# A decoder block in compensated fp32r: the second feed-forward block by seven block products, its hidden through memory, its last pass token tile by token tile

## The chip, the core and the metric

The kernel runs on one core of one Trainium2 chip. The metric is the device time of one execution in microseconds. A profiled execution gives, for the same core, the span from the first to the last instruction and a trace of every instruction: TensorE (PE, and PEld for its weight loads), VectorE (DVE), ScalarE (ACT), GpSimd (POOL) and SyncE (SP), whose queue issues most of the DMAs.

## What is computed

One sequence of 1024 tokens, width 1024, passes one decoder block and a final norm; d_ff is 2752:

```python
def rms_norm(x, g):
    return x * lax.rsqrt(jnp.mean(x * x, -1, keepdims=True) + EPS) * g
def swiglu(x, w_gu, w_down):
    gate, up = jnp.split(x @ w_gu, 2, axis=-1)
    return (jax.nn.silu(gate) * up) @ w_down

h = x
h = h + 0.5 * swiglu(rms_norm(h, ffn1_norm), ffn1_w_gu, ffn1_w_down)
h = h + hybrid_mixer(rms_norm(h, mix_norm), ...)      # sparse attention + HGRN2, then @ w_out
h = h + 0.5 * swiglu(rms_norm(h, ffn2_norm), ffn2_w_gu, ffn2_w_down)
return rms_norm(h, final_norm)
```

Everything is float32. The mixer's attention compresses keys and values in blocks of 32 tokens (`compress`), selects blocks, and has a window branch; the change touches its norm, its compression and the second half of its `w_out`.

## The kernel before

**A product.** TensorE multiplies in fp32r. Each fp32 operand is split into a high part and a rest (`split`, L134: the high part on POOL or ACT, the rest on DVE, L137 to L141), and each product is three matmuls, high by high, high by low, low by high (`mm3`, L143; the lines L145, L146, L147). A matmul has 128 x 128 weights and 512 columns in the feed-forward blocks.

**Tiles.** Tokens go in two halves of 512, or 8 tiles `tt` of 128. d_ff goes in 22 column tiles `j` of 128, the last 64 wide; a tile j has a gate and an up part. Plain, one j costs 2 parts x 2 token halves x 8 contraction tiles x 3 = 96 matmuls.

**FFN1** computes j = 0 to 2 plain (`up_plain`, L503), j = 3 to 20 by seven block products of the 2 x 2 blocks (contraction halves by token halves) (`up_strassen`, L561: 84 matmuls per j), j = 21 by `up_last`. The seven products need combined x operands, XO 0 to 6 (`x_sums`), built once, and combined weight pieces, built per j on DVE and POOL (`up_pieces`), and their results are combined by DVE. `up_out` (L493) multiplies by the norm factor R, applies silu and stores the hidden (`hs`) to memory by SP (L501). The second half, `down` (L594), makes four passes (token half x column half) over the 22 j; each pass reloads the hidden (L605) and w_down (L607), splits both, and accumulates four results; j = 0 and 1 are prepared in memory of their own ahead of the first pass. The norm of FFN1 needs each token's sum of squares: ACT squares xt, DVE adds (L215), 16 one-column matmuls sum over partitions (L221), rsqrt (L156 to L168), and L243 spreads the factors.

**Norms elsewhere** (`norm_rows`, L176): four whole-tile squares on ACT (L182), a rsqrt of 12 small DVE steps, four scaled tiles `xn` (DVE L192 twice, ACT, POOL L190), then transposes on TensorE (L201).

**FFN2** uses `ffn` (L324): chunks of two j, gate and up plain, the hidden stays on the chip; per chunk 16 results (8 token tiles x 2 column halves) of up to 6 matmuls (L405 to L407), each added to h by DVE (L409). After the last chunk come squares, rsqrt and output per token tile (L1426 to L1439).

**Order.** A scheduler sets the order within each engine from data and buffers; each engine then runs its list in that order, and a DMA queue too. So what stands behind a waiting instruction waits with it.

## Time and profile before

| what | value |
|---|---|
| median of 3 runs | 2183.11 us (2182.26 to 2185.56) |
| profiled execution, its own time | 2181.18 us |
| its span | 2179.5 us |
| mean granted TensorE clock | 0.995 |
| busy: PE, DVE, ACT, POOL | 98%, 57%, 27%, 21% |
| FFN1's first half ends, `down` ends | 438 us, 686 us |
| FFN2 starts, its last chunk's products start | 1451 us, 2140 us |

Engines run side by side and wait for each other by semaphores; a busy share is a mean over all stages. In a timeline row stand start, duration, engine, line, operation, what it writes and reads, and in brackets the idle time of that engine before it with what ended it. xN behind a row says that N like instructions are shown as one. A matmul's duration is longer than the distance from one start to the next, since matmuls are pipelined.

### The profile page before, as it was taken

The numbers are of one execution on the slowest core, as the hardware profiler recorded it, in microseconds if no ns is written. First come the engines' busy times: TensorE is split into PE (matmuls) and PEld (weight loads), VectorE is DVE, ScalarE is ACT, GpSimd is POOL, SyncE is SP. The second block draws the span as 40 slices with busy tenths as digits, with TensorE's granted clock in tenths as the row PEclk, the third lists the DMA queues.
The fourth block names the chain that finished last, engine by engine and source line by source line (L and its number), as shares of the span: only waits on it lengthen the run. The fifth ranks groups of instructions, "written<-read, shape, count | busy, mean of one in ns | idle before, by whom it ended". The sixth has DMA issues, their size and how long they took to land.

```text
span 2179.5 us, 29005 instructions
## 1 busy us (share of the span) xinstructions
PE 2134.0 (98%) x10866; PEld 1743.3 (80%) x10866; DVE 1231.6 (57%) x2560; ACT 589.6 (27%) x1270; POOL 461.7 (21%) x515
## 2 busy tenths in 40 slices
PE   8999999999999999999999999999999999999996
PEld 6888888878887889999866766698888888888884
DVE  8965555456775556556589776374333434333436
ACT  5532333222323111221576554330000000000003
POOL 2222223232231000001255333121010101010103
PEclk9999999999999999999999999999999999999998
DMA  5322222076773211100101111331111111111101
GB/s 174 98 77 78 87 88 82 34 292 194 229 239 105 81 39 40 42 20 20 39 20 38 41 42 37 131 117 57 40 46 52 49 49 58 40 48 49 45 9 78
DMA packets 87277, 169.14 MB, mean 78 GB/s; under 512 B 9792, under 2 KB 31328, under 8 KB 87136
## 3 DMA queue, kind: packets, MB, share of 16 engines
q1 hardware_dynamic: 85840, 163.07, 23.3%
q10 hardware_dynamic: 1296, 4.21, 0.5%
q8 instruction: 86, 1.41, 0.3%
q14 instruction: 55, 0.45, 0.1%
HBM read 145.49 MB, written 21.76 MB: 77 GB/s over the span
## 4 chain that ended last, share of the span: by engine, by line
PE 89%; DVE 6%; issue 2%; DMA 1%; ACT 1%; POOL 0%; SPq 0%; DVEq 0%; POOLq 0%; ACTq 0%
PE b L145 16%; PE b L147 16%; PE b L146 16%; PE b L1062 4%; PE b L620 4%; PE b L619 3%; PE b L618 3%; PE b L407 3%; PE b L405 3%; PE b L406 3%; PE b L1072 3%; PE b L638 2%; PE b L640 2%; PE b L639 2%; PE b L727 2%
## 5 line engine op out<-in xcount | busy, mean ns | idle before, releaser
L145 PE MATMUL b<-xT,wh 128*128 128x512 f32 x944 | 371.2, 394 | 0.8 <-DVE qa L921 0.7
L146 PE MATMUL b<-xT,wh 128*128 128x512 f32 x944 | 368.4, 390 | 0.0
L147 PE MATMUL b<-xT,wl 128*128 128x512 f32 x944 | 368.4, 390 | 0.0
L137 POOL TENSOR_SCALAR wh<-wr 128x1024 fp32r<-128x1024 f32 (+2 forms) x86 | 87.1, 1027 | 735.4 <-PE b L146 525.1
L145 PE MATMUL b<-xT,wp 128*128 128x512 f32 x584 | 228.4, 392 | 2.1 <-ACT pp L523 2.1
L146 PE MATMUL b<-xT,wp 128*128 128x512 f32 x584 | 228.1, 391 | 0.5 <-DVE xT L427 0.5
L147 PE MATMUL b<-xT,wp 128*128 128x512 f32 x584 | 227.8, 390 | 0.0
L341 DVE TENSOR_TENSOR sg<-b,sg 128x512 f32<-128x512 f32 (+1 forms) x44 | 30.4, 692 | 331.9 <-PE b L147 322.3
L147 PEld LDWEIGHTS b<-xT,wl 128*128 128x128 f32 x944 | 177.3, 188 | 37.4 <-issue 0.8
L145 PEld LDWEIGHTS b<-xT,wh 128*128 128x128 f32 x944 | 177.3, 188 | 36.0 <-POOL P L1041 0.8
L146 PEld LDWEIGHTS b<-xT,wh 128*128 128x128 f32 x944 | 177.5, 188 | 34.7
L141 DVE TENSOR_TENSOR dw<-dr,dw 128x512 fp32r<-128x512 f32 x172 | 133.5, 812 | 77.4 <-ACT dw L139 65.9
L409 DVE SCALAR_TENSOR_TENSOR g<-b,g 128x512 f32<-128x512 f32 x176 | 118.4, 685 | 59.8 <-PE b L407 59.6
L620 PE MATMUL b<-dw,dw 128*128 128x512 f32 x352 | 137.7, 391 | 0.2 <-DVE dw L141 0.2
L618 PE MATMUL b<-dw,dw 128*128 128x512 f32 x336 | 132.5, 394 | 5.1 <-POOL dw L137 4.3
L619 PE MATMUL b<-dw,dw 128*128 128x512 f32 x352 | 137.5, 391 | 0.0
L406 PE MATMUL b<-dh,hh 128*128 128x512 f32 x352 | 137.0, 389 | 0.0
L407 PE MATMUL b<-dl,hh 128*128 128x512 f32 x352 | 137.0, 389 | 0.0
L1041 POOL TENSOR_SCALAR P<-P,sm,gate 128x640 f32<-128x640 f32 (+7 forms) x128 | 106.3, 841 | 142.9 <-DVE sm L1039 138.8
L405 PE MATMUL b<-dh,hl 128*128 128x512 f32 x336 | 131.2, 390 | 5.1 <-DVE g L409 5.1
L141 DVE TENSOR_TENSOR wl<-wr,wh 128x1024 fp32r<-128x1024 f32 (+2 forms) x86 | 118.7, 1387 | 27.7 <-POOL wh L137 25.1
L1037 ACT ACTIVATE P<-P,sm 128x64 f32<-128x64 f32 (+8 forms) x192 | 114.8, 600 | 65.3 <-DVE sm L1002 57.0
(277 smaller groups left out, 4103.2 us busy)
## 6 DMA issues: line engine op xcount, KB each, us to landing
wr<-in_ffn_w_gu_dram SPq DMA_DIRECT2D x82, 512.0 KB, 3.7
dr<-in_ffn_w_down_dram SPq DMA_DIRECT2D x126, 256.0 KB, 3.1
dr<-hs SPq DMA_DIRECT2D x84, 256.0 KB, 3.1
hs<-sg SPq DMA_DIRECT2D x42, 256.0 KB, 2.2
wr<-in_w_in_dram SPq DMA_DIRECT2D x20, 512.0 KB, 5.0
wr<-in_w_out_dram SPq DMA_DIRECT2D x20, 256.0 KB, 3.1
xf<-in_xt_dram SPq DMA_DIRECT2D x16, 256.0 KB, 5.0
h<-in_x_dram SPq DMA_DIRECT2D x8, 512.0 KB, 6.4
```

The lines of the kernel that those rows point to most:

```text
L141: eng.tensor_tensor(out=lo, in0=src, in1=hi.bitcast(F32), op=OP.subtract)
L145: mm(ps, wh, xh, start=first, stop=False, skip_group_check=skip)
L146: mm(ps, wh, xl, start=False, stop=False, skip_group_check=skip)
L147: mm(ps, wl, xh, start=False, stop=last, skip_group_check=skip)
L405: mm(b[:], hl[:, c0:c0 + 128], dh[:], start=(j == js[0]), stop=False)
L406: mm(b[:], hh[:, c0:c0 + 128], dh[:], start=not hl and j == js[0], stop=False)
L407: mm(b[:], hh[:, c0:c0 + 128], dl[:], start=False, stop=(j == js[-1]))
L409: nc.vector.scalar_tensor_tensor(out=hv, in0=b[:], scalar=norm[1][:, tt:tt + 1] if norm else 0.5, in1=hv, op0=OP.mult, op1=OP.add)
L618: mm(bs[t][:], hl[:, c], dh[:], start=j == 0, stop=False)
L619: mm(bs[t][:], hh[:, c], dh[:], start=False, stop=False)
L620: mm(bs[t][:], hh[:, c], dl[:], start=False, stop=j == 21)
L1037: nc.scalar.activation(out=rng[br], in_=rng[br], func=AF.Exp, scale=-1.0, bias=m, accum_out=st[:, 6 + br:7 + br])
```

## The change

1. **FFN2** is computed as FFN1 is: j = 0 and 1 plain, j = 2 to 20 by seven products, j = 21 by `up_last`, the hidden through memory, then `down`. No factor R: x is normed before, so `up_out` lets ACT read the bank itself. x operands come from transposes (`x_cols`, and `x_cols2` for the second token half, with the combinations). h's rows 4 to 7 are stored to memory and all rows reloaded during the first pass of `down`.
2. **`down`**: three j instead of two are prepared ahead; in FFN2 the split operands have 16 buffers; in its last pass the last three j are done token tile by token tile, and `finish` adds, squares by half tiles, takes the rsqrt and stores each tile.
3. `up_last` stores its two results by ACT's queue instead of SP's, and its second output's products are on DVE, not POOL.
4. **FFN1's sums of squares** come from token-major rows of x (eight more loads of 512 KB on SP, ACT squares with accumulation); the additions and 16 one-column matmuls go.
5. **Squares in parts**: in FFN1's `down` per half tile as results come out; in w_out per 512 columns. w_out's second half reads its weights as 512-column pieces from the ring of FFN2's weights.
6. **Compression**: the flat tiles for keys and values get two buffers and are built between products.

```diff
-    def ffn(self, pool, wp, h, x, name, first, norm=None, early=None, mid=None, start=None, njt=22, chunk=2):
...
+    def square(self, pool, src, acc):
+        n = src.shape[-1]
+        junk = pool.tile([128, D], BF, name=self.nm("jk"), tag="jk", bufs=1)
+        self.nc.scalar.activation(out=junk[:, :n], in_=src, func=AF.Square, scale=D ** -0.5, accum_out=acc)
+    def normed(self, pool, rows, ss):
+        y = self.rsqrt(pool, ss[:, 0, :], 4, 1, "rs4", ss[:, 1, :])
+        return self.scale_rows(rows, [pool.tile([128, D], F32, name=self.nm("xn"), tag="xn", bufs=4) for _ in range(4)], y)
...
+    def x_cols2(self, rows, tag, gi, pool):
+        nc = self.nc
+        f = lambda o, kt: [self.XO[o][kt % 4 // 2][i][:, kt % 2, :].bitcast(F32) for i in range(2)]
+        tt = lambda o, a, b, op: nc.vector.tensor_tensor(out=o, in0=a, in1=b, op=op)
+        t = [pool.tile([128, 512], F32, name=self.nm("xs"), tag="xs", bufs=8)[:] for _ in range(KT)]
+        for kt in range(KT):
+            b = self.turned(rows, kt, tag)
+            g = self.gt[:, gi * KT + kt:gi * KT + kt + 1]
+            if kt < 4:
+                hi, lo = f(0, kt)
+                nc.vector.scalar_tensor_tensor(out=t[kt], in0=b[:], scalar=g, in1=hi, op0=OP.mult, op1=OP.subtract)
+                tt(t[kt], t[kt], lo, OP.subtract)
+                self.x_split(3, kt, t[kt])
+            else:
+                nc.scalar.activation(out=t[kt], in_=b[:], func=AF.Copy, scale=g)
+                self.x_split(2, kt, t[kt])
+            yield
+        for kt in range(4):
+            tt(t[kt], t[kt + 4], t[kt], OP.subtract)
+            self.x_split(4, kt, t[kt])
+        yield
...
     def up_out(self, cpool, g, u, R, dst, n=128, dve=False, queue=None):
-        e.tensor_tensor(out=s[:n], in0=g[:n], in1=R[:n], op=OP.mult)
-        nc.scalar.activation(out=s[:n], in_=s[:n], func=AF.Silu)
+        src = g[:n]
+        if R is not None:
+            e.tensor_tensor(out=s[:n], in0=src, in1=R[:n], op=OP.mult)
+            src = s[:n]
+        nc.scalar.activation(out=s[:n], in_=src, func=AF.Silu)
         e.tensor_tensor(out=s[:n], in0=s[:n], in1=u[:n], op=OP.mult)
-        nc.sync.dma_start(out=dst[:n], in_=s[:n])
+        (queue or nc.sync).dma_start(out=dst[:n], in_=s[:n])
...
-                p, nb = (pool, 5) if n == 0 and j < 2 else (pool2, 12)
+                early = n == 0 and j < 3
+                p, nb = (pool, 6) if early else (pool2, 11)
...
+                p, nb = (pool2, 16) if wide and not early else (pool, 12)
...
+                if n == 3 and j >= 22 - tail:
+                    left.append((j, hh, hl, dh, dl))
...
             for t in range(4):
+                for a in left:
+                    products(t, *a)
                 evac(half * 4 + t, ch, bs[t])
...
+        for tt in range(NT):
+            nc.sync.dma_start(out=rows[tt], in_=x[tt * 128:(tt + 1) * 128, :])
         for kt in (0, 4, 1, 5, 2, 6, 3, 7):
             lx(kt, 1)
...
+    def finish(tt, c, b):
+        hv = h[tt][:, c * 512:c * 512 + 512]
+        nc.vector.scalar_tensor_tensor(out=hv, in0=b[:], scalar=0.5, in1=hv, op0=OP.mult, op1=OP.add)
+        net.square(np_, hv, sq[tt][:, c:c + 1])
+        if c:
+            r = net.rsqrt(np_, sq[tt][:, 0:1], 1, 1, "rs", sq[tt][:, 1:2])
+            y = np_.tile([128, D], F32, name=net.nm("y"), tag="y", bufs=4)
+            for i in range(2):
+                k = slice(i * 512, i * 512 + 512)
+                nc.vector.scalar_tensor_tensor(out=y[:, k], in0=h[tt][:, k], scalar=r, in1=net.gb[:, k], op0=OP.mult, op1=OP.mult)
+                (nc.sync if i and tt >= 4 else nc.scalar).dma_start(out=out[0, tt * 128:(tt + 1) * 128, k], in_=y[:, k])
+    net.down(f2, f2b, "ffn2", H, finish, after, True, 3)
```

The changed kernel's lines have other numbers: L466 is the store of the hidden, L589 and L591 the reloads, L580 to L582 the products of `down`, L1476 and L1483 the addition and the output in `finish`.

Before, SP's list at the end of FFN1's first half (`hs` the hidden in memory, `sg` a result, `dr` a reload for column tile 2 and the next):

```order
L501 DMA hs_41_126<-sg_635_3345 128x512
L501 DMA hs_40_125<-sg_638_3367 128x512
L501 DMA hs_43_128<-sg_645_3455 128x512
L501 DMA hs_42_127<-sg_646_3473 128x512
L501 DMA hs_44_129<-sg_655_3540 64x512
L501 DMA hs_45_130<-sg_657_3548 64x512
L605 DMA dr_675_3629<-hs_6_91 128x512
L607 DMA dr_674_3628<-in_ffn1_w_down_dram 128x512
L605 DMA dr_681_3653<-hs_8_93 128x512
L607 DMA dr_680_3652<-in_ffn1_w_down_dram 128x512
```

And in the changed kernel, the same place of SP:

```order
L466 DMA hs_41_126<-sg_635_3325 128x512
L466 DMA hs_40_125<-sg_638_3347 128x512
L466 DMA hs_43_128<-sg_645_3435 128x512
L466 DMA hs_42_127<-sg_646_3453 128x512
L589 DMA dr_681_3635<-hs_8_93 128x512
L591 DMA dr_680_3634<-in_ffn1_w_down_dram 128x512
L1236 DMA h0_3548<-in_x_dram 128x1024
L589 DMA dr_687_3660<-hs_10_95 128x512
L591 DMA dr_686_3659<-in_ffn1_w_down_dram 128x512
```

The last two stores, of 64 rows, are no longer on SP; the reloads that follow the full stores are of column tile 3 (`hs_8`), since tiles 0 to 2 stand earlier in the list.

Before, TensorE's last matmuls (two results of FFN2's last chunk; `hl` and `hh` the hidden's parts, `dh` and `dl` those of w_down):

```order
L405 MATMUL b_3181_17930<-dh_3156_17808,hl_3144_17731 128x512
L406 MATMUL b_3181_17930<-dh_3156_17808,hh_3143_17730 128x512
L407 MATMUL b_3181_17930<-dl_3157_17809,hh_3143_17730 128x512
L406 MATMUL b_3181_17930<-dh_3159_17815,hh_3154_17803 128x512
L407 MATMUL b_3181_17930<-dl_3160_17816,hh_3154_17803 128x512
L405 MATMUL b_3182_17937<-dh_3162_17821,hl_3144_17731 128x512
L406 MATMUL b_3182_17937<-dh_3162_17821,hh_3143_17730 128x512
L407 MATMUL b_3182_17937<-dl_3163_17822,hh_3143_17730 128x512
L406 MATMUL b_3182_17937<-dh_3165_17828,hh_3154_17803 128x512
L407 MATMUL b_3182_17937<-dl_3166_17829,hh_3154_17803 128x512
```

In the changed kernel, the last but one tile of the last pass and the start of the last tile (`b` the bank, `dw` parts of hidden and weights of column tiles 19 to 21):

```order
L580 MATMUL b_3645_18549<-dw_3765_19013,dw_3764_19012 128x512
L581 MATMUL b_3645_18549<-dw_3765_19013,dw_3763_19011 128x512
L582 MATMUL b_3645_18549<-dw_3766_19014,dw_3763_19011 128x512
L580 MATMUL b_3645_18549<-dw_3771_19025,dw_3770_19024 128x512
L581 MATMUL b_3645_18549<-dw_3771_19025,dw_3769_19023 128x512
L582 MATMUL b_3645_18549<-dw_3772_19026,dw_3769_19023 128x512
L581 MATMUL b_3645_18549<-dw_3776_19037,dw_3775_19036 128x512
L582 MATMUL b_3645_18549<-dw_3777_19038,dw_3775_19036 128x512
L580 MATMUL b_3646_18550<-dw_3765_19013,dw_3764_19012 128x512
L581 MATMUL b_3646_18550<-dw_3765_19013,dw_3763_19011 128x512
```

Five matmuls of two column tiles ended a result before; now eight of three column tiles end it, and the 57 of the first 19 column tiles stand earlier in the list, among those of the other three tiles.

Before, VectorE at FFN2's head (`g7` the last addition of w_out, `wl` the rest of a weight split, `xT` x's rest, `rs4` the rsqrt):

```order
L1398 TENSOR_TENSOR g6_12935<-b_2545_13454,g6_12935 128x256
L205 SCALAR_TENSOR_TENSOR xT_2498_12962<-b_2546_13480,gt_137,xT_2497_12961 128x512
L1398 TENSOR_TENSOR g7_12937<-b_2547_13487,g7_12937 128x256
L141 TENSOR_TENSOR wl_2586_13735<-wr_2587_13736,wh_2585_13734 128x1024
L205 SCALAR_TENSOR_TENSOR xT_2498_12962<-b_2548_13513,gt_137,xT_2497_12961 128x512
L156 TENSOR_SCALAR rs4_2562_13543<-ss4_2557_13534 128x4
L141 TENSOR_TENSOR wl_2586_13735<-wr_2588_13737,wh_2585_13734 128x1024
L159 TENSOR_SCALAR rs4_2562_13543<-rs4_2562_13543 128x4
L161 TENSOR_SCALAR rs4_2562_13543<-rs4_2562_13543 128x4
L166 TENSOR_TENSOR rs4_2562_13543<-rs4_2562_13543 128x4
```

In the changed kernel (`ws` a combination of weight tile 2 from its loads `wr_2671`, `wp` the rest of a split of tile 1, `sq` the sums of squares):

```order
L438 TENSOR_TENSOR ws_2698_14044<-ws_2697_14043,wr_2671_13855 128x512
L1397 TENSOR_TENSOR g5_12927<-b_2573_13463,g5_12927 128x256
L329 SCALAR_TENSOR_TENSOR xT_2498_12955<-b_2575_13491,gt_137,xT_2497_12954 128x512
L1397 TENSOR_TENSOR g6_12928<-b_2576_13498,g6_12928 128x256
L329 SCALAR_TENSOR_TENSOR xT_2500_12957<-b_2578_13526,gt_137,xT_2499_12956 128x512
L141 TENSOR_TENSOR wp_2638_13699<-wr_2628_13617,wp_2637_13698 128x512
L141 TENSOR_TENSOR wp_2640_13703<-wr_2628_13617,wp_2639_13702 128x512
L141 TENSOR_TENSOR wp_2642_13707<-wr_2629_13618,wp_2641_13706 128x512
L1397 TENSOR_TENSOR g7_12929<-b_2579_13533,g7_12929 128x256
L141 TENSOR_TENSOR wp_2644_13711<-wr_2629_13618,wp_2643_13710 128x512
L329 SCALAR_TENSOR_TENSOR xT_2500_12957<-b_2581_13561,gt_137,xT_2499_12956 128x512
L158 SCALAR_TENSOR_TENSOR rs4_2630_13621<-sq_13089 128x4
```

The combination of weight tile 2 stands ahead of the last three additions, and the splits of four weight pieces stand around the last of them; the rsqrt comes after the additions as before.

## Rows read from the trace of the kernel before

**Rows 1.** The profile page: busy time of each engine, share of the span, instructions.

```profile
PE 2134.0 (98%) x10866; PEld 1743.3 (80%) x10866; DVE 1231.6 (57%) x2560; ACT 589.6 (27%) x1270; POOL 461.7 (21%) x515
```

**Rows 2.** Busy time by stretch: us, PE, PEld, DVE, ACT, POOL, PEclk, DMA share, GB/s.

```profile
100.00:440.00 340.00, 340.00 (x1502) 281.62 (x1501) 187.19 (x288) 101.10 (x170) 95.45 (x72) 1.00 0.25 75
452.00:590.00 138.00, 138.00 (x616) 114.23 (x615) 91.11 (x129) 39.66 (x64) 38.95 (x53) 1.00 0.75 252
1500.00:2140.00 640.00, 640.00 (x2825) 530.14 (x2824) 245.50 (x317) 48.01 (x79) 66.69 (x77) 1.00 0.14 44
2140.00:2165.00 25.00, 19.88 (x83) 14.47 (x81) 22.89 (x55) 11.60 (x18) 13.27 (x6) 1.00 0.16 63
```

**Rows 3.** Timeline, 2140 to 2180: start, duration, engine, line, operation, idle before.

```profile
2140.29 0.39 PE L405 MATMUL b<-dh,hl 128*128 128x512 f32 x1
...
2162.93 13.74 SPq L1439 DMA_DIRECT2D out_dram<-y  x8
...
2164.60 0.39 PE L407 MATMUL b<-dl,hh 128*128 128x512 f32 x1
...
2165.96 0.68 DVE L409 SCALAR_TENSOR_TENSOR g<-b,g 128x512 f32<-128x512 f32 x1
...
2170.45 0.63 ACT L1426 ACTIVATE jk<-g 128x512 bf16<-128x512 f32 x1 [0.90 <-DVE rs L168]
...
2174.90 1.41 DVE L1437 SCALAR_TENSOR_TENSOR y<-g,rs,gb 128x512 f32<-128x512 f32 x2
```

**Rows 4.** Waits, 2135 to 2180: total us, times, longest.

```profile
PE b L405 <- DVE g L409: 5.1, 3, 1.7
```

**Rows 5.** Timeline around the end of FFN1's first stage, 441 to 452.

```profile
443.08 0.45 SPq L501 DMA_DIRECT2D hs<-sg  x1
...
443.58 0.39 PE L620 MATMUL b<-dw,dw 128*128 128x512 f32 x1
...
448.27 0.80 PE L618 MATMUL b<-dw,dw 128*128 128x512 f32 x1 [4.31 <-POOL dw L137]
...
451.43 0.42 PE L619 MATMUL b<-dw,dw 128*128 128x512 f32 x1
```

**Rows 6.** Timeline of the norm ahead of the mixer, 685 to 701.

```profile
689.25 1.06 ACT L182 ACTIVATE jk<-h 128x1024 bf16<-128x1024 f32 x1 [10.43 <-DMA hspill<-h]
...
695.32 0.17 DVE L156 TENSOR_SCALAR rs<-ss 128x4 f32<-128x4 f32 x1 [7.90 <-ACT jk L182]
...
698.30 0.87 PE L201 MATMUL b<-ident,xn 128*128 128x128 f32 x6 [1.61 <-DVE xn L192]
```

**Rows 7.** Waits of TensorE, 690 to 800.

```profile
PE b L201 <- DVE xn L192: 2.3, 2, 1.6
...
PE b L852 <- DMA w<-in_cmp_v_w_dram: 1.9, 1, 1.9
...
PE b L852 <- DVE fl L843: 1.6, 1, 1.6
```

**Rows 8.** Timeline of FFN1's head, 20 to 40.

```profile
23.93 3.85 POOL L137 TENSOR_SCALAR wx<-wr 128x512 fp32r<-128x512 f32 x4 [4.62 <-DMA wr<-in_ffn_w_gu_dram]
...
29.22 0.94 PE L221 MATMUL b<-ones,acc 128*128 128x1 f32 x8
...
38.45 2.07 PE L243 MATMUL b<-dg,ones 128*128 128x512 f32 x2 [3.59 <-DVE dg L236]
```

**Rows 9.** All transfers of the first 26 us.

```profile
DMA packets 4527, 8.24 MB, mean 317 GB/s; under 512 B 727, under 2 KB 1751, under 8 KB 4527
```

**Rows 10.** VectorE and GpSimd, second half of w_out and FFN2's head.

```profile
1423.50 1.22 DVE L141 TENSOR_TENSOR wl<-wr,wh 128x1024 fp32r<-128x1024 f32 x1
...
1438.73 2.05 DVE L141 TENSOR_TENSOR wl<-wr,wh 128x1024 fp32r<-128x1024 f32 x1 [0.77 <-POOL wh L137]
...
1437.64 2.06 POOL L137 TENSOR_SCALAR wh<-wr 128x1024 fp32r<-128x1024 f32 x2 [5.64 <-PE b L640]
...
1457.73 2.29 DVE L192 TENSOR_SCALAR xn<-g,rs 128x1024 f32<-128x1024 f32 x2
```

More of the change, by code (lines that the diff above doesn't have):

```diff
@@ L1238, in body @@
     h = [hp.tile([128, D], F32, name=f"h{tt}") for tt in range(NT)]
-    f2b = pool(cf, "f2b", "right")
+    sq = [np_.tile([128, 2, 4], F32, name=f"sq{half}") for half in range(2)]
     Y, after = {}, {}
@@ new lines, in body @@
+    next(plain)
+    for o in range(2):
+        net.up_simple(wu, ws, 1, raws[1], o=o)
+    net.x_operand(xp, 3)
+    net.x_operand(xp, 2)
+    cols = net.x_cols2(rows, "b", 2, xf)
+    for _ in range(4):
+        next(cols)
+    next(plain)
+    for _ in range(4):
+        next(cols)
+    next(plain)
+    cr.close()
+    xq = pool(cu, "xq2", "right")
+    net.xbufs[id(xq)] = 12
+    raws.update({j: net.up_raw(wu, name, j) for j in (2, 3)})
+    next(plain)
+    next(plain)
+    net.x_operand(xq, 4)
@@ new lines, in body @@
+    next(cols)
+    next(plain)
+    net.x_operand(xq, 5)
+    net.x_operand(xq, 6)
+    next(cols)
+    rest = net.up_rest(wu, ct, name, 2, raws, None, H)
+    next(rest)
+    cx.close()
+    f2 = pool(cd, "f3")
+    next(rest)
+    cu.close()
+    f2b = pool(ctx, "f3b", "right")
+    hp = pool(ctx, "h3", "right")
+    np_ = pool(ctx, "n3", "right")
+    net.load_gain(ins["final_norm"][None, :])
+    h = [hp.tile([128, D], F32, name=f"k{tt}") for tt in range(NT)]
+    sq = [np_.tile([128, 2], F32, name=f"sk{tt}") for tt in range(NT)]
@@ new lines, in body, with reload @@
+    after = {}
+    def reload(tt):
+        with net.late():
+            nc.sync.dma_start(out=h[tt][:], in_=spilled(tt))
+    for tt in range(NT):
+        after[0, 2 * tt + 3] = lambda tt=tt: reload(tt)
+    def finish(tt, c, b):
[9 more added lines that the diff above has]
+                (nc.sync if i and tt >= 4 else nc.scalar).dma_start(out=out[0, tt * 128:(tt + 1) * 128, k], in_=y[:, k])
```

454 lines of the change are left out of this document (200 added, 254 removed).

## The prediction

> **What bounds the kernel now.** I read the page first, then busy time by stretch, then the waits and the timeline at each seam between stages. TensorE is busy for 98% of the span and no other engine for more than 57% [rows 1]: time goes down only if TensorE issues less, or if a seam at which it stands still closes. Inside the feed-forward stages there is nothing to close. FFN2's long stretch is busy 640.00 of 640 us with 2825 matmuls, so one costs 640/2825 = 0.2265 us from start to start, though each lasts 0.39; FFN1's stretch of seven products, which is what FFN2 becomes, is 340.00 of 340 us at 340/1502 = 0.2264, with VectorE at 55%, ScalarE at 30% and GpSimd at 28% [rows 2]. The seams are the end [rows 3, 4], FFN1's passage from its first to its second half [rows 5], the norm and the compression in the mixer [rows 6, 7] and FFN1's head [rows 8]. All sums are made against the profiled execution, 2181.2 us (span 2179.5 and 1.7 around it); the median of the three runs is 2183.1.
>
> **A. Fewer products.** 19 of FFN2's 22 column tiles go from 96 to 84 matmuls: 19 x 12 = 228, and 228 x 0.2265 = **-51.6**. The other engines pay for it: every tile costs weight combinations, splits and seven result combinations, but FFN1's same work fills 55% of VectorE, and FFN2's is lighter by one multiplication per output. So it lies beside TensorE [rows 2].
>
> **B. The end.** Before, the last chunk has 80 matmuls (16 results of 5): 80 x 0.2265 = 18.1, but from 2140.29 to 2164.99 it takes 24.7, since each result must be added to h by VectorE before its bank is free (three waits on L409 [rows 4], and each late start costs more): 6.6 lost. After, 4 tiles end the last pass, each 8 matmuls (3 column tiles, the last a half) = 1.81 us, and VectorE adds one result per 1.81: **-6.6**. Then the tail. Before, the last matmul ends at 2164.99 and the span at 2179.5: 14.5. After, counted from the last matmul: 0.97 to the add (2164.99 to 2165.96), 0.68 for it, a square of 0.63 plus its reading; meanwhile VectorE finishes the rsqrt of tiles 5, 6 and 7 and three outputs at 1.41 for two halves, which puts the last output's end at +8.6; from the last output to the end of the span it is 2179.5 - 2176.3 = 3.2. So 11.8, **-2.7**. Bounds: the last tile's own chain alone would be about 9.6 (-5), a queue of rsqrts as now gives 0.
>
> **C. FFN1 from first to second half.** Before, TensorE issues at 443.58, next at 448.27, then 7 matmuls up to 451.43 at 0.45 apiece instead of 0.2265: 448.27 - 443.58 - 0.23 = 4.46, and 3.16 - 1.59 = 1.57, together 6.0 [rows 5]. The reason is the queue: SP's last store of the hidden waited for GpSimd's product until 443.08, and the loads of column tile 2 stand behind it. After, the last two stores are on ScalarE's queue, and three column tiles instead of two are ready, 3 x 12 x 0.2265 = 8.2 us of products for loads that took 448.27 - 443.08 = 5.2 from store to product. **-6.0** (0 if the loads instead wait for their buffers to come free). FFN2 has the same passage now; I take 0 for it, between -0 and the +6 measured here. On ScalarE's queue the stores stand ahead of that engine's splits for the second half; only the third column tile's would wait, and it has 5.4 us.
>
> **D. FFN1's head.** Eight loads of x, 4.19 MB, go ahead of the second half of xt and of weight tile 2. The first 26 us move 8.24 MB at 317 GB/s in the mean [rows 9], some 380 once going, so tile 2, which GpSimd began to split at 23.93 [rows 8], lands about 11 us later, at 35. TensorE now does tile 1 before it, has work until then, and idles earlier instead, while it waits for tile 1. What goes is the 16 small matmuls (0.9 for eight in [rows 8], twice in all) and the 3.59 for which L243 waits at 38.45, because the sums no longer hang on TensorE and on 14 additions of VectorE. I come out at **-1.7**; bounds: -4 (all of the wait) to +4 (tile 2 late by a third of 11 us).
>
> **E. The norm ahead of the mixer.** Before, four whole squares start at 689.25 and the rsqrt at 695.32, and TensorE waits at 698.30 and once more, 2.3 in all [rows 6, 7]. After, the squares are taken half a tile at a time as results come out; only the last half is left. **-2.3** (-3 to 0). **F. Compression.** TensorE waits 1.6 for the flat tiles and 1.9 for weights [rows 7]; with both tiles built ahead the first goes, the second partly: **-2** (-3.5 to 0).
>
> **G. FFN2's head** is what costs. w_out's second half transposes the first half's rows already during its third part; the rsqrt there now stands behind the splits of the 512-column weight pieces on VectorE, and TensorE's queue reaches the transpose in order: about +2. At the end VectorE's order has two combinations of weight tile 2, which wait for a transfer, ahead of the last three additions and of the second rsqrt; TensorE comes to the transposes 24 matmuls (5.4 us) after w_out, when 2.2 of rsqrt (12 small steps at some 0.18, the first of such a chain lasts 0.17 in [rows 6]), 2.3 for two rows [rows 10], the square and the handoffs leave about 1: +1.5. The operands of the second token half come after that: about 50 VectorE operations at 0.69, some 34 us, against five groups of 24 to 48 plain matmuls that hide them. By hand operand 2 is early by 7 us, operand 4 too, operand 6 by 1. **+3.5** (0 to +8).
>
> A row speaks against that cover: the same VectorE subtraction of 128x1024 takes 1.22 at 1423.50 and 2.05 at 1438.73, beside two GpSimd splits that run from 1437.64 [rows 10]. The Trainium skill (SBUF — State Buffer, section "Who interferes with whom") says that a VectorE instruction with two inputs in SBUF contends with a GpSimd instruction that reads SBUF, and that whoever is second waits. The trace agrees in kind, with a factor of 2.05/1.22 = 1.7. By the rule every subtraction that meets a GpSimd split would stretch so, which is rival 1 with its 2122; by what I lay beside them few meet one, which is the sum here.
>
> **H.** Between the passes of a second half the banks change hands, and FFN2 adds a square and the reload of h: +0.5 (0 to +3).
>
> Sum: -51.6 - 6.6 - 2.7 - 6.0 - 1.7 - 2.3 - 2 + 3.5 + 0.5 = -68.9; 2181.2 - 68.9 = 2112.3. The runs' median lies 1.9 above the profiled run, so I say **2113**. All ends at their best give 2101.
>
> **Rivals.** (1) FFN2's head is not covered. If a third to a half of those 50 operations run at 1.7 times 0.69, VectorE is later by 8 to 12 us than by my sum, more than the 1 to 7 it has in hand, and TensorE waits once for operand 5 or 6: about 2122. For it: [rows 10]; against: in that stretch GpSimd has little but the splits of two weight tiles. (2) Only the products and the end pay, and the other seams stay or move to a neighbour, as waits tend to (C, D, E and F at nothing): 2181.2 - 51.6 - 9.3 + 4 = 2124. For it: each of them is a chain whose next link is late soon after. (3) FFN1's head goes the wrong way, by +4 rather than -1.7: 2118. (4) Slower: FFN2's second half is bound by memory. Its four passes reload hidden and weights, 22 x 2 x 256 KB each, some 45 MB, within the 1040 x 0.2265 = 236 us of their products, where the old chunks loaded only weights. To eat the 69 us they would have to take 305 us, below 148 GB/s. Against: FFN1's second half, the same code, is busy 138.00 of 138 us at 252 GB/s [rows 2]. (5) The change doesn't take the products out: the instruction order shows TensorE with 228 fewer, so this is all but excluded.
>
> **Numbers.** Forecast 0.62 (own range 2106 to 2118), rival 1 0.15, rival 2 0.13, rival 3 0.07, rival 4 0.02, rival 5 0.01. The range runs from the best ends, 2101, to just past rival 2, 2126. About 0.2% is what can be told from no change here (4 us): every case but rivals 4 and 5 is far below it, so faster 0.97, same 0.01, slower 0.02.
>
> **What would show it.** In the profile after: TensorE with 228 fewer matmuls of 512 columns in FFN2; a stretch of FFN2 with no idle at 0.2265 per matmul; at the end about 12 us from last matmul to end of span; no gap of more than 1 us at either passage from first to second half; the waits on L201's successor and on the flat tiles gone from the list. It is wrong if TensorE waits over 5 us in the first 60 us of FFN2 (rival 1), if those passages still show 4 us (rival 2), or if the clock or the transfers make a matmul of FFN2's second half cost more than 0.23.

## The result, and the profile after

The changed kernel takes 2118.99 us (median of 4 runs, 2117.99 to 2121.74) beside 2183.09 for the kernel before (2182.26 to 2185.56): a ratio of 0.9707 with a 95% interval of 0.9690 to 0.9723. The forecast was 2113. The profiled execution took 2118.82 us with a span of 2117.1, so against the profiled run of before the span fell by 62.4 where the sum had 68.9.

Seven stages, cut at the same instructions in both traces (TensorE's start of one to its start of the next, the tail from the end of the last matmul), show where the 62.4 came from:

| stage | before | after | difference | predicted |
|---|---|---|---|---|
| start to end of FFN1's plain tiles | 84.76 | 82.87 | -1.9 | -1.7 (D) |
| FFN1's tiles of seven products and the last tile | 353.60 | 355.16 | +1.6 | nothing |
| FFN1's second half | 247.29 | 242.08 | -5.2 | -6.0 (C) |
| mixer, up to w_out's second half | 715.07 | 711.26 | -3.8 | -4.3 (E, F) |
| w_out's second half | 49.86 | 53.39 | +3.5 | +2 (G) |
| FFN2 | 714.40 | 661.42 | -53.0 | -56.2 (A, last chunk of B, +1.5 of G, H) |
| tail | 14.48 | 10.92 | -3.6 | -2.7 (rest of B) |

The first two rows together are FFN1's first half, 438.36 and 438.03. The same code measured again in other kernels gives 241.2 to 243.9 in the third row, 711.1 to 713.4 in the fourth and 52.3 to 54.3 in the fifth, so a difference of under about 2.5 us there tells little from one run.

The page's first row after, which answers to [rows 1]:

```profile
PE 2080.7 (98%) x10622; PEld 1698.3 (80%) x10622; DVE 1317.3 (62%) x2754; ACT 724.1 (34%) x1523; POOL 510.3 (24%) x576
```

TensorE is still the engine with the least idle time; the others do more, and have room for it. Busy time by stretch of the kernel after (us, then PE, PEld, DVE, ACT, POOL, granted clock, DMA share, GB/s), beside [rows 2]:

```profile
430.00:470.00 40.00, 40.00 (x179) 33.10 (x178) 21.78 (x29) 8.71 (x14) 9.43 (x13) 1.00 0.87 306
1495.00:1868.00 373.00, 372.67 (x1644) 308.29 (x1643) 193.36 (x292) 115.75 (x193) 76.77 (x61) 1.00 0.27 84
1868.00:2106.00 238.00, 236.63 (x1041) 194.74 (x1039) 151.16 (x246) 63.53 (x114) 58.71 (x82) 1.00 0.64 207
1445.00:2106.00 661.00, 658.12 (x2912) 542.69 (x2910) 388.12 (x614) 203.37 (x348) 139.94 (x147) 1.00 0.39 127
```

The same view of the kernel before, all of FFN2:

```profile
1451.00:2165.00 714.00, 708.86 (x3138) 585.39 (x3136) 290.10 (x407) 73.32 (x117) 87.10 (x89) 1.00 0.14 45
```

FFN2 has 3138 - 2912 = 226 fewer matmul records (228 by the order). 372.67/1644 = 0.2267 us each in the first half and 238.00/1041 = 0.2286 in the second, at 207 GB/s: the second half is bound by its matmuls, not by memory. The first row is the passage in FFN1, where [rows 5] had the gap: 40.00 of 40 us.

The end, a timeline of the kernel after, beside [rows 3]:

```profile
2105.79 0.39 PE L582 MATMUL b<-dw,dw 128*128 128x512 f32 x1
...
2106.67 0.69 DVE L1476 SCALAR_TENSOR_TENSOR k<-b,k 128x512 f32<-128x512 f32 x1
...
2112.75 1.42 DVE L1483 SCALAR_TENSOR_TENSOR y<-k,rs,gb 128x512 f32<-128x512 f32 x2
```

The last matmul ends at 2106.18 and the last output 8.0 later (the sum had 8.6), then 2.9 to the end. The waits of TensorE after, first in the mixer, then from 1400 to 1470, then in all of FFN2, three answers, which stand beside [rows 4, 7] (total us, times, longest):

```profile
PE b L849 <- DMA w<-in_cmp_v_w_dram: 2.2, 2, 2.0
```

```profile
PE b L199 <- DVE xn L187: 3.1, 3, 1.9
```

```profile
PE b L580 <- DVE dw L141: 0.9, 1, 0.9
PE b L145 <- POOL xn L185: 0.6, 1, 0.6
PE b L199 <- DVE xn L187: 0.6, 1, 0.6
```

The waits for the flat tiles (1.6) and for the norm ahead of the mixer (2.3) are gone, the latter since only the last half-tile square is left of the squares that the chain waited for [rows 6]; the wait for weights stays, at 2.2 (1.9 before). The wait on scaled rows (L201 before, L199 now) has gone to w_out and FFN2's head: 3.1, where it was 0.5.

FFN1's head after, beside [rows 8]: timeline rows of TensorE and GpSimd.

```profile
17.39 0.79 PE L145 MATMUL b<-xT,wp 128*128 128x512 f32 x1 [5.38 <-POOL wp L137]
...
34.88 1.20 POOL L137 TENSOR_SCALAR wx<-wr 128x512 fp32r<-128x512 f32 x2 [14.93 <-DMA wr<-in_ffn_w_gu_dram]
...
36.87 1.12 PE L232 MATMUL b<-dg,ones 128*128 128x512 f32 x2 [0.45 <-DVE dg L225]
```

The wait of 3.59 for the factors has shrunk to 0.45, and tile 2 begins to be split at 34.88, where the sum put it ("at 35"). But TensorE now stands 5.38 us at 17.39, before tile 1, where in the kernel before it had stood 2.06 at 13.78 (its waits, 0 to 60 us):

```profile
PE b L145 <- ACT pp L523: 2.1, 1, 2.1
```

All the same it is ahead when FFN1's plain tiles end. The first matmul of the seven products, before and then after:

```profile
84.76 0.39 PE L145 MATMUL b<-xT,wp 128*128 128x512 f32 x1
```

```profile
82.87 0.39 PE L145 MATMUL b<-xT,wp 128*128 128x512 f32 x1
```

So the head gained 1.9, and most of it was lost again at one place in the first tile of seven products, where the kernel before had no wait. VectorE and TensorE of the kernel after:

```profile
99.28 0.68 DVE L141 TENSOR_TENSOR dw<-dr,dw 128x512 fp32r<-128x512 f32 x1
99.88 0.68 DVE L555 TENSOR_TENSOR pd<-b,pd 128x512 f32<-128x512 f32 x1
...
100.61 0.50 PE L145 MATMUL b<-xT,wp 128*128 128x512 f32 x1 [1.26 <-DVE pd L555]
```

The addition for which TensorE waits (L555) stands on VectorE behind splits of `down`'s column tiles prepared ahead (`dw`): six of them between 92.28 and 99.96, where two tiles took four. The first 26 us move as much as in [rows 9]:

```profile
DMA packets 3881, 8.31 MB, mean 319 GB/s; under 512 B 551, under 2 KB 1575, under 8 KB 3880
```

### The profile page after: what moved, and what is told of

Same layout as the page of the kernel before. It is cut to its first block, busy times and chain, and to the rows that moved or that the text cites. A ratio compares the mean times of both kernels' runs of the same rounds, so it can differ in the third digit from the quotient of the medians.

```text
span 2117.1 us, 30083 instructions
## 1 busy us (share of the span) xinstructions
PE 2080.7 (98%) x10622; PEld 1698.3 (80%) x10622; DVE 1317.3 (62%) x2754; ACT 724.1 (34%) x1523; POOL 510.3 (24%) x576
## 5 line engine op out<-in xcount | busy, mean ns | idle before, releaser
L145 PE MATMUL b<-xT,wp 128*128 128x512 f32 x1196 | 467.4, 391 | 7.6 <-POOL wp L137 5.4
L146 PE MATMUL b<-xT,wp 128*128 128x512 f32 x1196 | 466.4, 390 | 0.3 <-DVE xT L329 0.2
L147 PE MATMUL b<-xT,wp 128*128 128x512 f32 x1196 | 466.1, 390 | 0.0
L141 DVE TENSOR_TENSOR dw<-dr,dw 128x512 fp32r<-128x512 f32 x344 | 263.6, 801 | 152.2 <-ACT dw L139 128.5
L582 PE MATMUL b<-dw,dw 128*128 128x512 f32 x704 | 274.2, 390 | 0.7 <-DVE dw L141 0.7
L581 PE MATMUL b<-dw,dw 128*128 128x512 f32 x704 | 274.0, 389 | 0.0
L145 PEld LDWEIGHTS b<-xT,wp 128*128 128x128 f32 x1196 | 225.1, 188 | 56.7 <-POOL wp L137 6.5
L580 PE MATMUL b<-dw,dw 128*128 128x512 f32 x672 | 262.3, 390 | 2.3 <-DVE dw L141 2.3
L146 PEld LDWEIGHTS b<-xT,wp 128*128 128x128 f32 x1196 | 224.9, 188 | 47.7 <-DVE xT L329 1.3
L147 PEld LDWEIGHTS b<-xT,wp 128*128 128x128 f32 x1196 | 224.9, 188 | 47.2 <-DVE wp L141 0.4
L139 ACT ACTIVATE dw<-dr 128x512 fp32r<-128x512 f32 x168 | 105.6, 631 | 308.5 <-PE b L580 199.1
L137 POOL TENSOR_SCALAR dw<-dr 128x512 fp32r<-128x512 f32 x176 | 125.7, 715 | 348.6 <-PE b L582 244.4
L139 ACT ACTIVATE wp<-ws 128x512 fp32r<-128x512 f32 x148 | 93.2, 631 | 243.3 <-PE b L146 237.7
L141 DVE TENSOR_TENSOR wp<-ws,wp 128x512 fp32r<-128x512 f32 x148 | 103.7, 702 | 85.9 <-ACT wp L139 85.7
L582 PEld LDWEIGHTS b<-dw,dw 128*128 128x128 f32 x704 | 132.0, 188 | 29.7 <-DVE dw L141 2.2
L581 PEld LDWEIGHTS b<-dw,dw 128*128 128x128 f32 x704 | 132.2, 188 | 27.2
L580 PEld LDWEIGHTS b<-dw,dw 128*128 128x128 f32 x672 | 126.1, 188 | 29.2 <-POOL dw L137 1.8
L141 DVE TENSOR_TENSOR wp<-wr,wp 128x512 fp32r<-128x512 f32 (+1 forms) x155 | 110.2, 722 | 18.2 <-ACT wp L139 15.0
```

Of the source, the lines that this page charges most:

```text
L137: nc.gpsimd.tensor_scalar(out=hi, in0=src, scalar1=1.0, scalar2=1.0, op0=OP.mult, op1=OP.mult)
L139: nc.scalar.activation(out=hi, in_=src, func=AF.Copy)
L141: eng.tensor_tensor(out=lo, in0=src, in1=hi.bitcast(F32), op=OP.subtract)
L145: mm(ps, wh, xh, start=first, stop=False, skip_group_check=skip)
L146: mm(ps, wh, xl, start=False, stop=False, skip_group_check=skip)
L147: mm(ps, wl, xh, start=False, stop=last, skip_group_check=skip)
```

## The experiments

The theory to be tested: TensorE's own count sets FFN2; C's gap was the store queue; the ends and heads are chains whose next link was mis-sized. Line numbers in the variants are up to 8 higher, by their edits. All are read by the stages above; each variant ran once, except `final`.

### Is TensorE alone the bound of FFN2's first half?

`six` drops one of the seven products in FFN2:

```diff
-        self.up_mm(Q[:], w[6], 6, False, True)
+        if R is not None:
+            self.up_mm(Q[:], w[6], 6, False, True)
```

> Leaves out the seventh block product of FFN2's 19 column tiles j = 2 to 20 (12 matmuls each; its result's addition stays and reads an older bank), so FFN2's gate and up results are not the reference's. Theory (TensorE alone bounds FFN2's first stage, so a matmul taken out is worth its 0.2265 us): 228 x 0.2265 = 51.6 us less than the changed kernel's 2117.1 us span, so 2065.5. Rival (VectorE, GpSimd or the transfers are close behind and take over): less than 40 us gained, and TensorE shows waits between 1500 and 1820.

FFN2's first half went from 423.28 to 370.89, -52.4, with 2069.84 for the whole. A stretch of it, by the same view as above:

```profile
1500.00:1819.00 319.00, 319.00 (x1409) 264.16 (x1408) 217.84 (x290) 113.45 (x193) 82.04 (x58) 1.00 0.27 94
```

With 228 more matmuls gone TensorE is still busy without a break at 319/1409 = 0.2264, though VectorE is up to 68%. The price per product is shown, and that nothing else stood within these 52 us behind it.

`dve8` goes the other way, eight more VectorE additions of 128x512 per tile (152 in all), results unused:

```diff
+                    for _ in range(2):
+                        nc.vector.tensor_tensor(out=self.idle[:], in0=p[:], in1=p[:], op=OP.add)
```

> Adds 8 idle VectorE additions of 128x512 to each of FFN2's 19 seven-product tiles, 152 x 0.69 = 105 us of work on VectorE, spread over the middle of the tile. Theory (VectorE's work there lies beside TensorE with room: 52% busy now, 80% with it): at most 1 to 2 us slower than 2117.1. Rival (the cover is thin, since the combined results and weight pieces are handed on in order): over 10 us slower, with TensorE waiting for VectorE in every tile.

```profile
1495.00:1871.00 376.00, 374.01 (x1644) 309.27 (x1643) 298.94 (x445) 115.75 (x193) 87.64 (x61) 1.00 0.26 84
```

```profile
1513.39 0.50 PE L145 MATMUL b<-xT,wp 128*128 128x512 f32 x1 [1.99 <-DVE pd L563]
```

VectorE took 298.94 - 193.36 = 105.6 us more and reached 80%; FFN2's first half grew by 3.1, and 2.0 of it is this one wait, in the first tile of seven products, where VectorE is busy without a break. Elsewhere the work is hidden but for the 1.1 that is left. The theory held, a little undersized (1 to 2 expected).

### What closed the gap in FFN1's passage?

C named one reason, the store that SP's queue had ahead of the loads. Three edits act there: the store on ScalarE's queue with its second product on VectorE, a third tile prepared ahead, and, not spoken of in the prediction, that the buffers for `down`'s later tiles (`f2b`) are laid out ahead of h's rows and no longer behind them. `both2` undoes the first two, `place` the third alone, `both2p` all three.

```diff
-        self.up_out(cpool, V, u, R, H[j][0], 64, True, nc.scalar)
+        self.up_out(cpool, V, u, R, H[j][0], 64, True)
...
-        self.up_out(cpool, p, u, R, H[j][1], 64, True, nc.scalar)
+        self.up_out(cpool, p, u, R, H[j][1], 64)
...
-                early = n == 0 and j < 3
+                early = n == 0 and j < 2
```

> Both feed-forward blocks pass from the first to the second half as before the change: two column tiles prepared ahead instead of three, the last two stores of the hidden on SP's queue, the second output's product on GpSimd. Theory (that passage cost 6.0 us in FFN1 and would in FFN2): 8 to 12 us slower than 2117.1, half of it at each passage. Rival (the new place of the buffers, free at the end of the first half, closed the gap): at most 2 us slower.

```diff
-    f2b = pool(cf, "f2b", "right")
     hp = pool(cf, "h1", "right")
...
     h = [hp.tile([128, D], F32, name=f"h{tt}") for tt in range(NT)]
+    f2b = pool(cf, "f2b", "right")
```

> FFN1's buffers for the reloads (f2b) are taken after h again, as before the change, so that they lie where the last results of FFN1's first half (ct) lay; the rest is the changed kernel. Theory (three prepared column tiles and ScalarE's queue for the last stores close the passage by themselves): the time from the end of FFN1's first half to the end of its second half stays within 1.5 us of 242.1. Rival (the place of the buffers closed it, since a reload into a result's memory must wait for that result's store): 3 us or more longer, with TensorE waiting about 8 us after the first half's end.

> All three of the passage's edits undone in FFN1: two prepared column tiles, last stores on SP's queue with the product on GpSimd, and f2b after h. Theory: FFN1's passage is as before the change, a gap of 4 to 5 us in TensorE some 5 us after the end of the first half and slower matmuls after it, 6 us in all, so that FFN1's second half goes from 242.1 to 248 us; with f2b in its new place (both2) the gap was 1.2 us only. Rival (the gap of before came from something else, as the order of the mixer's tables on GpSimd): no more than the 1.2 us of both2.

The stretch from 430 to 470 in `both2`, `place` and `both2p`, to be set beside 40.00 (x179) after:

```profile
430.00:470.00 40.00, 38.84 (x167) 30.50 (x166) 22.66 (x27) 8.44 (x15) 13.70 (x15) 1.00 0.77 276
```

```profile
430.00:470.00 40.00, 37.52 (x164) 30.00 (x163) 18.95 (x27) 7.79 (x13) 11.17 (x12) 1.00 0.70 252
```

```profile
430.00:470.00 40.00, 35.57 (x150) 28.65 (x149) 18.81 (x25) 7.57 (x12) 13.35 (x14) 0.96 0.71 262
```

In matmul records that is 12, 15 and 29 fewer, at 0.2265 each 2.7, 3.4 and 6.6 us; in the ten kernels that leave the passage alone no start in it is late. The second half of FFN1 took 246.19, 245.18 and 247.98 beside 242.08. `both2` was expected at 8 to 12 and gave 4.1 there and 0.5 in FFN2: a miss, and more than its rival's 2. `place` lost 3.1, as its rival said (3 or more). Only with all three undone is the old gap back (`both2p`, TensorE):

```profile
447.13 0.50 PE L580 MATMUL b<-dw,dw 128*128 128x512 f32 x1 [4.43 <-POOL dw L137]
```

Before it was 4.31 [rows 5]. The mechanism of the third edit is in SP's queue: the first reload behind the last full store, in the kernel after and then in `place` (start, duration):

```profile
430.10 0.32 SPq L589 DMA_DIRECT2D dr<-hs  x1
```

```profile
440.15 0.32 SPq L589 DMA_DIRECT2D dr<-hs  x1
```

Nothing but the buffers' place differs, and the load starts ten us later. What it waited for is in the waits of SP's queue in `place`, from 424 to 456:

```profile
SPq L589 <- DVE sg L462: 10.8, 1, 10.8
```

It is VectorE's multiplication of the last result by the norm factor (L462, at 439.37): the memory that the load is to fill was still in use. So C's gap had two causes of about equal size, the queue with the number of tiles ahead (2.7) and the buffers (3.4), and together they make up the whole. How much of the 2.7 is the queue's and how much the third tile's was not told apart.

The third tile has a price of its own, which `both2` and `both2p` show beside their purpose. The stretch from the first matmul of the seven products to the end of FFN1's first half is 355.2 to 356.1 in the nine kernels with three tiles ahead and the changed kernel's head, each with a wait of TensorE for L555's addition near 100 us; with two tiles ahead it is 353.9 in `both2`, without that wait, and 354.5 in `both2p`, with 0.55 of it. (`headp` and `headq`, whose plain tiles end later, have three tiles with 0.42 and none of the wait.) So the third tile's splits cost FFN1's first half some 1 to 2 us.

### The tail

`tail0` gives up the token-tile order of the last pass (last argument 3 to 0):

```diff
-    net.down(f2, f2b, "ffn2", H, finish, after, True, 3)
+    net.down(f2, f2b, "ffn2", H, finish, after, True, 0)
```

> FFN2's last pass keeps its old order: the last three column tiles are not done token tile by token tile. Theory (the end is VectorE's queue: four additions, four rsqrt chains and eight output halves, one after the other): the four results end within 1.8 us of each other, VectorE then needs 4 x (0.68 + 1.4 + 1.41) = 14 us, and with 1 us before and 3 us of output transfer the time from the last matmul to the end of the span goes from 10.9 to 17 to 18 us: 6 to 7 us slower. Rival (the end is one tile's own chain and the output transfer): at most 2 us slower.

```profile
2106.91 1.89 DVE L1476 SCALAR_TENSOR_TENSOR k<-b,k 128x512 f32<-128x512 f32 x3 [6.91 <-PE b L582]
...
2107.84 0.39 PE L582 MATMUL b<-dw,dw 128*128 128x512 f32 x1
...
2117.26 1.42 DVE L1483 SCALAR_TENSOR_TENSOR y<-k,rs,gb 128x512 f32<-128x512 f32 x2
```

The tail is 13.37 instead of 10.92: +2.5, not the 6 to 7 expected, and not the rival's 2 at most either. Two things were mis-sized. The additions were expected 1 us behind the last matmul's end (2108.23), but the first starts 1.3 ahead of it. And VectorE's stretch from there to the end of the last output is 11.8 us where 14 were expected: four additions (2.6) and four outputs (5.6) leave 3.6 for the four rsqrt chains, which run through each other, instead of 4 x 1.4. The tile order is worth 2.5 us.

`tailp` takes the second output half of tiles 4 to 6 off VectorE (ScalarE scales, GpSimd multiplies by the gain):

```diff
+                if i and 4 <= tt < 7:
+                    nc.scalar.activation(out=y[:, k], in_=h[tt][:, k], func=AF.Copy, scale=r)
+                    nc.gpsimd.tensor_tensor(out=y[:, k], in0=y[:, k], in1=net.gb[:, k], op=OP.mult)
```

> In the last pass the second output half of token tiles 4, 5 and 6 is scaled by ScalarE and multiplied by the gain on GpSimd instead of VectorE. Theory (after the last product VectorE's queue is what lasts, and tile 7's rsqrt stands behind the outputs of 5 and 6): 2 to 3 halves of 0.66 us go from that queue, so the time from the last matmul to the end of the span goes from 10.9 to 9.5 us (9 to 10). Rival (tile 7's own chain and the output transfer set the end, as tail0's small loss suggests): 10.5 us or more, or longer because the halves on GpSimd come last.

Tail 11.49, +0.6: the theory's 9.5 did not come. The last output starts at 2113.30 instead of 2112.75 though VectorE has three operations of 0.7 fewer. That does not make the rival right, since the edit also held VectorE up. VectorE and GpSimd of `tailp`:

```profile
2108.94 1.31 DVE L164 SCALAR_TENSOR_TENSOR rs<-rs 128x1 f32<-128x1 f32 x1
2108.98 1.26 POOL L1485 TENSOR_TENSOR y<-y,gb 128x512 f32<-128x512 f32 x1 [2.38 <-ACT y L1484]
```

A step of the rsqrt that takes 0.21 elsewhere lasts 1.31 here and ends with GpSimd's multiplication; at 2111.86 it happens again (1.21, beside a multiplication from 2111.79 to 2113.05). Without these 2.1 us the tail would be about 9.4, an estimate from these rows. Whether VectorE's work or the chain of tile 7 sets the end stays open.

### FFN1's head

`headp` runs the second half of tile 0's contraction first, loads weight tile 2 ahead of the second half of xt, and issues the scalings of xt late:

```diff
+                        with (self.tc.issue_after(pe[mybir.EngineType.PE]) if pe else nullcontext()):
...
+        raws[2] = net.up_raw(wu, "ffn1_w_gu", 2)
         for kt in (0, 4, 1, 5, 2, 6, 3, 7):
...
-        next(sums)
+        with net.late():
+            next(sums)
```

> FFN1's head reordered: TensorE does the second contraction half of column tile 0 ahead of all of tile 1, ScalarE's scalings of x wait, and the loads of weight tile 2 go ahead of the second half of xt. Theory (in the changed kernel TensorE stands 5.4 us at 17 us for tile 1 while ready work is queued behind it, and after that tile 2 comes late): the gap at 17 us falls below 3 us, and FFN1's first half ends 2 us (1 to 3.5) earlier than 438.0. Rival (the head is bound by the 4 MB of loads ahead of the second half of xt, so any time won is lost again where the second half's operands are needed): first half ends within 0.7 us of 438.0, with a new wait between 40 and 60 us.

The stall of 5.38 fell to 3.01, but the first half ended at 440.07, 2.0 later. Two rows of ScalarE and TensorE:

```profile
29.58 0.58 ACT L491 ACTIVATE pp<-b 128x512 f32<-128x512 f32 x1
...
30.31 0.76 PE L150 MATMUL b<-xT,wp 128*128 128x512 f32 x1 [3.96 <-ACT pp L491]
```

The copy that frees TensorE's bank stood behind eight squares on ScalarE (19.36 to 29.5). `headq` therefore gives the squares in groups of 4, 2 and 2 between the products:

```diff
+        squares(0, 4)
         next(plain)
+        squares(4, 6)
+        next(plain)
+        squares(6, 8)
```

> As headp, but ScalarE squares the rows of x in three groups (4, 2, 2), with the copies out of TensorE's banks for column tile 1 between them, so that no copy stands behind a square that waits for its row. Theory (headp lost its gain to that queue: a copy issued at 29.6 behind eight squares, TensorE waiting 4.0 us for it): headp's wait at 30 us is gone or below 1 us, and the first half ends 1.5 to 3 us before the changed kernel's 438.0. Rival (the head is bound by its 12 MB of loads, whatever the order): the first half ends at 437.5 or later, with the wait at another place between 24 and 60 us.

It ended at 444.37, worse still. ScalarE and TensorE:

```profile
39.24 0.20 ACT L665 ACTIVATE lbe<-lbe 128x4 f32<-128x4 f32 x1 [8.34 <-DVE lbe L664]
...
43.87 2.08 PE L237 MATMUL b<-dg,ones 128*128 128x512 f32 x2 [10.56 <-DVE dg L230]
```

Now a small operation of the mixer (L665), which waits for a late load, stood ahead of the last square (39.35), and the whole chain square, rsqrt, factors behind that. Both attempts failed by what an in-order engine had in front, not by the idea; whether a clean order of the head would gain is open.

### The seam from w_out to FFN2

G put its two waits down to work that stands ahead of the norm's chain on VectorE. `seam` begins the transposes one token tile later and puts the combinations of weight tile 2 behind the second norm:

```diff
-            if cq >= 2:
+            if cq == 3 or cq == 2 and i:
...
-    next(rest)
+    with net.late(m):
+        next(rest)
```

> Two edits at the end of w_out. The transposes of the first token half start one token tile later, so that their rows are ready; and VectorE, ScalarE and GpSimd combine weight tile 2 only after the second norm's rows. Theory (TensorE's waits of 2.7 us at 1420 and of 1.1 us at 1451 come from the order of the queues, not from a lack of engine time): both waits fall below 0.5 us each, 3 to 4 us gained by the end of FFN2's first stage. Rival (the wait moves: the operands of FFN2's first tiles, or weight tile 2's pieces, come late instead): a new wait of 2 us or more between 1445 and 1515.

w_out's second half fell from 53.39 to 50.17, but the waits at FFN2's head stayed (0.7 and 0.6 for the scaled rows) and FFN2's first half took 0.6 more (0.4 of it four transposes that moved there), since the last addition (1445.63) still stood behind splits of weight tile 1 (1443.61, 2.10 us for two). `seam2` adds to it:

```diff
-    for o in range(2):
-        net.up_simple(wu, ws, 1, raws[1], o=o)
+    with net.late({mybir.EngineType.DVE: m[mybir.EngineType.DVE]}):
+        for o in range(2):
+            net.up_simple(wu, ws, 1, raws[1], o=o)
```

> As seam, and VectorE splits FFN2's weight tile 1 only after the second norm's rows too, so that nothing but x's own columns stands ahead of w_out's last additions. Theory (in seam the last addition of w_out still waited behind three splits on VectorE until 1445.6, some 2 us after its product): TensorE's wait of 1.5 us at the second norm's transposes falls below 0.5, and w_out's and FFN2's first stage together are 4 us shorter than in the changed kernel (764.65 + 423.27). Rival (the rsqrt chain and the row scalings take 4.5 us by themselves and are what TensorE waits for): the wait stays at 1 us or more, or tile 1's weights make TensorE wait at 1455 to 1460.

The waits of TensorE from 1400 to 1470, `seam` and then `seam2`:

```profile
PE b L204 <- DVE xn L192: 1.5, 2, 0.8
PE b L150 <- POOL xn L190: 0.6, 1, 0.6
```

```profile
PE b L204 <- DVE xn L192: 0.8, 1, 0.8
PE b L204 <- DVE xs L379: 0.3, 1, 0.3
```

w_out's second half is 50.05 and FFN2's first half 422.74, together 3.9 less than after; with the rest of the mixer, as the expectation counts, 3.7 (4 expected). The same kernel was timed against the kernel before as `final`:

> The kernel of seam2 again, timed against the kernel before in five rounds. Theory (its two waits fewer are worth 3.7 us of w_out and FFN2's first stage, and nothing else moved): 0.969 of the kernel before, some 0.0015 below the changed kernel's 0.9707. Rival (the 3 us of seam2's one look were the run's, not the edit's): 0.9705 or more.

2116.89 (2113.49 to 2120.34, 5 runs) against 2185.56: a ratio of 0.9684 with an interval of 0.9671 to 0.9697. Its point lies 0.0023 below the change's own 0.9707, but the intervals overlap: that it beats the kernel before is shown, that it beats the changed one in whole time is not. In its own stage it does: w_out's second half is 50.2, 50.1 and 50.8 in the three kernels with the edit (`seam`, `seam2`, `final`) and 52.3 to 54.3 in the ten without it; 0.4 of the difference are the four transposes.

## Why the prediction was right, and where it was not

The forecast's mechanism, fewer products behind an otherwise covered FFN2, is what happened, and the time came 6 us above it. That is 1 us outside the forecast's own range (2106 to 2118) and next to rival 3's 2118, so the time alone doesn't tell the forecast from its rivals; the stages do. The sum ends at 2112.3 for the profiled run, against 2118.8; with the 1.9 by which the runs' median lay higher it would have said 2114, not 2113. The stages add up to the gap: -0.2 (D), +1.6 (FFN1's seven products, in no term), +0.8 (C), +0.5 (E, F), +1.5 (first part of G), +3.2 (FFN2), -0.9 (tail) = 6.5.

**A and the last chunk** hold. 228 matmuls at 0.2265 are 51.6, and `six` measured 52.4 for as many again. With the 6.6 of the last chunk 58.2 were to go, 53.0 went, so the new FFN2 has 5.2 of its own losses. The terms G and H allowed 1.5 + 0.5 of it.

**H was undersized**: the second half needs 1040 x 0.2265 = 235.6 and took 238.15, 2.5 more instead of 0.5. Most of it is one place, some 8 us into the third pass (which starts at 1985.90), where the splits are late. VectorE and TensorE of the kernel after:

```profile
1996.09 1.41 DVE L1483 SCALAR_TENSOR_TENSOR y<-k,rs,gb 128x512 f32<-128x512 f32 x2
...
1997.49 0.68 DVE L141 TENSOR_TENSOR dw<-dr,dw 128x512 fp32r<-128x512 f32 x1
...
1998.32 0.47 PE L580 MATMUL b<-dw,dw 128*128 128x512 f32 x1 [0.86 <-DVE dw L141]
```

From 1994.29 to 1999.65 there are 14 steps in 5.36 us, 2.2 over 14 x 0.2265. The second pass completes token tiles 0 to 3, and VectorE has their rsqrt chains and outputs (L1483) among the third pass's splits (L141). The term counted a square and the reload of h there, and put these chains and outputs at nothing; no variant moved them.

**G's second part** was +1.5 and came out at about 5.2 - 2.5 = 2.7. The cause that the sum named: combinations and splits of weights ahead of the last addition. What the sum left out is how long splits last there. VectorE, and GpSimd beside it, at FFN2's head after:

```profile
1442.79 3.49 POOL L137 TENSOR_SCALAR wp<-wr 128x512 fp32r<-128x512 f32 x4 [5.28 <-issue]
...
1444.11 2.71 DVE L141 TENSOR_TENSOR wp<-wr,wp 128x512 fp32r<-128x512 f32 x3
...
1447.08 0.67 DVE L141 TENSOR_TENSOR wp<-wr,wp 128x512 fp32r<-128x512 f32 x1
```

Three splits beside GpSimd's take 0.90 each, the one after it 0.67: the stretch of [rows 10] again, at 1.3 instead of 1.7, just ahead of the chain (from 1448.34). But `seam2` and `final`, which moved that work, took only 0.5 of the 2.7 away, 0.9 without the four transposes that moved in; what holds the rest isn't shown. The first part, +2 in w_out, came as +3.5, of which 2.5 are waits on L199 (3.1 less the 0.6 in FFN2). The three variants took 2.6 to 3.3 of it, so this place is shown by experiment.

**E and F** hold: -3.8 of -4.3 up to w_out's second half (-1.6 to -4.0 in the nine other kernels with this mixer and w_out). The list of waits has -2.3 and -1.3 of it (3.5 before, 2.2 after, for F). The stage lost it again only at its end, by G's first part.

**C** had the right size, 5.2 of 6.0 in the stage, for a reason that was half of it. The step "the reason is the queue" fails: of some 6 us, 2.7 come from the queue and the tiles ahead, 3.4 from the place of the buffers, which the prediction had only as a bound ("if the loads instead wait for their buffers"). They would have waited, had the change not moved the buffers as well.

**D** holds, -1.9 of -1.7 by the end of the plain tiles (82.3 to 83.6 in the ten other kernels with this head, 84.76 before). The wait for factors went (3.59 to 0.45), the tile came at 34.88, and TensorE idles earlier, as the prediction said: 5.38 at 17.39 instead of 2.06 at 13.78. The sum's omission lies behind it: C's third column tile was booked for what it closes at the passage, and the splits that it puts on VectorE at 92 to 100 us were in no term. They cost the first tile of seven products 1 to 2 us, 1.6 in the changed kernel.

**B's tail** was better by 0.9: 0.6 ahead of the last output's end (8.0 instead of 8.6) and 0.3 in the transfer behind it (2.9 instead of 3.2). One link of the 0.6 was misread. The 0.97 from the last matmul to its addition is no distance between the engines: in the kernel before, VectorE was in a step of the rsqrt until 2166.04, held up beside GpSimd (the rows are at the end of this text). In the kernel after, the addition starts at 2106.67, 0.49 behind, when VectorE is done with the one before. What the other links gave isn't shown.

Of the rivals, 1 (a head that isn't covered, over 5 us of waits in 60) and 4 (memory) are refuted by the waits of FFN2 and by 207 GB/s at 0.2286, 5 by the count of matmuls; 2 describes what the third tile's splits and w_out took back, but not C, D, E, F and the tail; 3 went the other way (-1.9 at the end of the head).

## What to carry to other kernels

Price the work that moves, not only the wait that goes: the third tile's splits, w_out's second half, FFN2's head and the third pass lost 1 to 2 us each beyond the sum, in places where the profile before had little or no wait, and nearly all of the 6 us lies there. Cut a stage where its terms end: FFN1's first half as a whole moved by 0.3, which hid a gain of 1.9 and a loss of 1.6. Where a load seems held by a queue, ask for its buffer too: the edit that lets the load start can be the one that moves memory, and only undoing both tells. Where an engine runs a list in order, put what frees the bottleneck's bank or feeds its next operand ahead of what merely happens to be ready: the two failed heads broke this, and the seam that paid kept to it.
